# Weight-sum transfers in a one-core decoder trunk: plain copies on SyncE's queue, adds on GpSimd's, both held until 1/rms of their half

## The chip, the cores and the metric

The kernel runs on one core of one Trainium2 chip. The metric is the device time of one execution in microseconds (us), the median of the runs shown; lower is better.

## What is computed

One layer on x of shape (1, 2048, 1024), all in float32 (cut from the reference):

```python
h = rms_norm(x, norm1_g)
z = einsum('bsd,de->bse', h, w_in)            # 1024 -> 3584
lru_x, lru_gate, sc_b, sc_c, sc_x = split(z)
y_lru = rg_lru(causal_dwconv(lru_x, lru_conv_w) + lru_conv_b, ...) * gelu(lru_gate)
y_sc = sc_b * causal_dwconv(sc_c * sc_x, sc_conv_w)
x = x + einsum('bse,ed->bsd', concatenate([y_lru, y_sc]), w_out)
h = rms_norm(x, norm2_g)
gate, up = split(causal_dwconv(einsum('bsd,df->bsf', h, w_up), ffn_conv_w))
x = x + einsum('bsf,fd->bsd', gelu(gate) * up, w_down)
return rms_norm(x, final_g)
```

## The kernel before

Activations stand transposed, features on the 128 partitions and time along the free dimension. The 2048 positions are worked in two **halves** of 1024. Float32 products are made of three reduced-precision ones: `split` (L192 to L194) writes a high part with ScalarE and the rest with VectorE, and TensorE sums high x high, high x low and low x high.

The program goes through six stages in order: input phase of half 0 (`in_phase`, L403), output product of half 0 (`sweeps` named "o"), input phase of half 1, output product of half 1, then up product and down product of half 0, and up and down product of half 1. The order on TensorE (PE), SyncE (SP) and GpSimd (POOL) is that of the code; VectorE (DVE) and ScalarE (ACT) are ordered by a scheduler with priorities, so that an instruction more elsewhere can move theirs.

**Input phase.** It makes 28 input products a half, each of 48 matmuls of 128x512. `load_weights` puts the transfer of a product's weights (512 KB, `wr_in`, L211) on SP's queue into one of two raw buffers; eight of the products bring gate weights in the same raw buffer (L216), which stays taken until these are split. The products are not divided by the norm first: 1/rms of the half (`inv_rms`, L257 to L271, tile `ss_a`) is computed after the first products and multiplied in when a product leaves PSUM (`evac`, L362). What follows is convolution (L290, L292), gates (`zr`, `zi`), scan (L344), and stores of the result blocks to HBM (`y_d`, L190). `with_halo` and `keep_halo` (L276 to L283) are small GpSimd instructions that carry the last columns of a tile from half to half.

**Output and down product.** `sweeps` (L674) uses a Strassen-like scheme with seven block products instead of eight. Each sweep loads a weight block (L701) and a feature block (L702, from `y_d` or `f_d`), splits both, and runs 24 matmuls for each pair. In the output product of half 0, x of half 1 is loaded and prepared beside it (`x1_beside`, L391 to L393, `sq`, L246, L247); in that of half 1 it is the input of the up product (`h_beside`, L507). Both read 4 MB for this. The output product has 7 x 3 x 24 = 504 matmuls.

**Weight sums.** Four of the seven weight operands are sums of blocks: S1 = W21 + W22, S3 = W21 + W11, S2 = S1 + W11, S4 = S2 + W12. They are made by transfers from HBM to HBM of 512 KB each, without an engine: a plain copy into the sum's place (`so_d` for the output weights, `sd_d` for the down weights), then a transfer that adds the second operand there. There are 3 blocks a sum for `so_d` and 6 for `sd_d`, so 12 copies and 12 adds in half 0, and 24 and 24 in half 1. All are issued on GpSimd's queue in `in_product`, after each input product, one at a time in half 0 and two in half 1:

```python
for _ in range(min(half + 1 if o != 1 or half else 0, len(pieces))):   # L354
    dst, src, op = pieces.pop(0)
    nc.gpsimd.dma_start(dst, src, accum_op=op, max_dma_last_dim=2 * T)  # L356
```

`sums` (L662) makes the list `pieces`; that of the down weights is made right before the output product of half 0, so that its transfers belong to the input phase of half 1. GpSimd runs ahead of TensorE where nothing holds it.

Of the kernel before, what the change touches and what calls it, by code (L numbers as in the profile page):

```python
# [10 lines left out]
ALU = mybir.AluOpType  # L11
# [5 lines left out]
T = 1024  # L17
# [14 lines left out]
W_OPS = ["W21", "W11", "W22", "W12"]  # L32
# [19 lines left out]
]  # L52
PLACE = {"11": (0, 0), "12": (0, 1), "21": (1, 0), "22": (1, 1)}

SUMS = [("S1", "W21", "W22"), ("S3", "W21", "W11"), ("S2", "S1", "W11"), ("S4", "S2", "W12")]

O_G1, O_G2, O_GF = 0, 8, 16
O_LCW = 24
# [10 lines left out]
def block_kernel(  # L69
# [11 lines left out]
    nc = tc.nc  # L81
# [9 lines left out]
    ones = cp.tile([P, P], F32, name="ones")  # L91
# [22 lines left out]
    def col(o):  # L114
        return prm[:, o : o + 1]
# [4 lines left out]
    def act(name):  # L120
        return page(name, "act", 28)
# [4 lines left out]
    def tmp(name):  # L126
        return page(name, "tmp", 7)
# [7 lines left out]
    def pst(name):  # L135
        return pp.tile([P, NB], F32, name=name, tag="ps")
# [4 lines left out]
    def flat(t):  # L141
        return t.rearrange("p a b -> p (a b)")

    def r32(ap):
        return ap.bitcast(F32R)

    def blk(b):
        return slice(b * NB, (b + 1) * NB)
# [28 lines left out]

    waiting = []
    pieces = []

    def defer(n, dst, src):
        waiting.append([n, dst, src])
# [66 lines left out]
    def mean_split(acc, name):  # L249
        n = acc.shape[-1]  # L250
        hi = flat(tmp(f"rh_{name}"))[:, :n]
        lo = flat(tmp(f"rl_{name}"))[:, :n]
        with tc.high_priority(offset=HP):
            split(hi, lo, acc)
        return hi, lo

    def inv_rms(acc, name, parts=None):  # L257
        n = acc.shape[-1]
        terms = parts or mean_split(acc, name)
        pss = [pst(f"ms_{name}_{t}") for t in range(0, n, NB)]  # L260
        for i, x in enumerate(terms):
            for b, p in enumerate(pss):
                nc.tensor.matmul(p, ones_r, r32(x[:, blk(b)]), start=i == 0, stop=i == len(terms) - 1)
        with tc.high_priority(offset=HP):
            y = flat(tmp(f"ry_{name}"))[:, :n]
            for b, p in enumerate(pss):
                nc.scalar.activation(y[:, blk(b)], p, AF.Abs_reciprocal_sqrt, bias=eps)
                nc.vector.scalar_tensor_tensor(acc[:, blk(b)], p, EPS, y[:, blk(b)], ALU.add, ALU.mult)  # L268
            nc.vector.scalar_tensor_tensor(acc, acc, -0.5, y, ALU.mult, ALU.mult)
            nc.vector.scalar_tensor_tensor(acc, acc, 1.5, y, ALU.add, ALU.mult)  # L270
        return acc  # L271

    def with_halo(name, n, half, store, side):
        t = big(name, side)
        if half == 0:
            nc.gpsimd.memset(t[:, 0:n], 0.0)  # L276
        else:
            nc.gpsimd.tensor_copy(t[:, 0:n], store)
        return t

    def keep_halo(t, n, half, store):
        if half < NH - 1:
            nc.gpsimd.tensor_copy(store, t[:, T : T + n])  # L283
# [12 lines left out]
    def lru_conv(c, half, ps, rs):  # L296
        xl = with_halo(f"xl{half}_{c}", 3, half, xl_halo[:, c, :], c % 2)
        evac(xl[:, 3 : 3 + T], ps, rs)
        keep_halo(xl, 3, half, xl_halo[:, c, :])
        cv = flat(act(f"cv{half}_{c}"))  # L300
        conv(cv, xl, 4, O_LCW + 4 * c, bias=col(O_LCB + c))
        xc = (flat(act(f"xch{half}_{c}")), flat(act(f"xcl{half}_{c}")))
        split(xc[0], xc[1], cv)
        return xc, cv
# [22 lines left out]
    def lru_scan(c, half, cv, g, ps_r, ps_i):  # L327
# [20 lines left out]
        nc.vector.tensor_tensor(h, g, h, ALU.mult)  # L348
        return h

    def in_product(o, half, acts):
        ps = pst2(f"zin{half}_{o}")
        product(ps, load_weights(w_in[o], f"in{half}_{o}", o - NLRU if NLRU <= o < 2 * NLRU else None), acts)
        for _ in range(min(half + 1 if o != 1 or half else 0, len(pieces))):  # L354
            dst, src, op = pieces.pop(0)
            nc.gpsimd.dma_start(dst, src, accum_op=op, max_dma_last_dim=2 * T)  # L356
        return ps

    def evac(dst, ps, rs):
        with tc.high_priority(offset=HP):  # L360
            for b, p in enumerate(ps):
                nc.vector.tensor_tensor(dst[:, blk(b)], p, rs[:, blk(b)], ALU.mult)  # L362
# [40 lines left out]
    def in_phase(half, acts, acc, between):  # L403
# [19 lines left out]
        gw = gate_weights(0, half)  # L423
        ps_2 = in_product(1, half, acts) if half == 0 else None
        rs = inv_rms(acc, f"a{half}", parts)
        xc, cv = lru_conv(0, half, pss[0], rs)
        if half == 0:
            decay_rates()
# [231 lines left out]
            between(j)  # L660

    def sums(src, dst, n):  # L662
        for k in range(2 * len(SUMS)):
            o, a, b = SUMS[k // 2]
            for i2 in range(n // 2):
                t = flat(dst[o][i2])
                if k % 2 == 1:
                    pieces.append((t, src[W_OPS.index(b), i2], ALU.add))
                elif a in W_OPS:
                    pieces.append((t, src[W_OPS.index(a), i2], ALU.bypass))  # L670
                else:
                    pieces.append((t, flat(dst[a][i2]), ALU.bypass))

    def sweeps(half, wsrc, fsrc, ni, name, residual, done, beside, tail=0):  # L674
        keep = None
# [69 lines left out]
    ss1[0] = acc_tile("a0")  # L745
    sums(w_out, so_d, NO)
    in_phase(0, None, ss1[0], nothing)
    assert not pieces
    sums(w_down, sd_d, NI)

    x1 = []
# [240 lines left out]
```

## Time and profile before

| | |
|---|---|
| median of 3 runs (lowest to highest) | 2332.79 us (2329.52 to 2335.15) |
| the profiled execution | 2334.91 us, of which the span from first to last instruction 2333.1 us |
| TensorE busy, mean granted clock | 98% of the span, 0.989 |
| VectorE, ScalarE, GpSimd busy | 74%, 49%, 7% |
| transfers | 378.28 MB; SP's queue 41.8% and GpSimd's 7.5% of 16 engines' span |

Busy shares are of the whole span; a stage in which TensorE waits shows in the slices of the span and in tables by stretch. Queue q1 (hardware) is SP's, q0 (software) GpSimd's. A matmul's mean duration overlaps the next one's; the distance of two starts is what it costs.

### The profile page before, as it was taken

How to read it: one execution, taken by the hardware profiler on the slowest of the kernel's cores; microseconds unless marked ns; L12 is line 12 of the kernel's file. 1: busy time of each engine (PE TensorE's matmuls, PEld its weight loads, DVE VectorE, ACT ScalarE, POOL GpSimd, SP SyncE). 2: the span in 40 equal slices, each digit the busy share in tenths (PEclk: the TensorE clock that was granted, in tenths of full speed). 3: DMA queues.
4: the chain of work that ended last, by engine and by line, in shares of the span. 5: the costliest groups of instructions: out<-in, count | busy, mean ns of one | idle time of the engine just before them, and what ended most of it. 6: DMA issues, size and time to landing. Idle time of an engine off the chain costs nothing.

```text
span 2333.1 us, 26007 instructions
## 1 busy us (share of the span) xinstructions
PE 2283.3 (98%) x9984; PEld 1880.7 (81%) x9984; DVE 1724.3 (74%) x1910; ACT 1136.7 (49%) x1242; POOL 167.0 (7%) x266
## 2 busy tenths in 40 slices
PE   8999997999999999999999999999999999999997
PEld 7888885778888878888888888888888888887885
DVE  7656566757666699898887877677888887876656
ACT  5553464536525645554444454445454444443343
POOL 0001110101110000020111100000010001100000
PEclk9999998999999999999999999999999999999999
DMA  4344448966763288232323247576223232348754
GB/s 160 98 126 124 127 115 312 286 213 151 183 166 91 96 291 294 98 113 91 114 91 123 94 149 283 189 247 240 101 91 113 91 113 91 113 163 314 258 193 180
DMA packets 149629, 378.28 MB, mean 162 GB/s; under 512 B 13824, under 2 KB 17024, under 8 KB 149504
## 3 DMA queue, kind: packets, MB, share of 16 engines
q1 hardware_dynamic: 134528, 338.87, 41.8%
q0 software_dynamic: 14976, 37.75, 7.5%
q8 instruction: 78, 1.28, 0.2%
q14 instruction: 47, 0.39, 0.1%
HBM read 289.53 MB, written 124.78 MB: 178 GB/s over the span
## 4 chain that ended last, share of the span: by engine, by line
PE 74%; DMA 6%; DVE 6%; ACT 2%; issue 1%; SPq 0%; POOL 0%; DVEq 0%; ACTq 0%; POOLq 0%
PE zx L569 22%; PE zin_b L232 13%; PE zc L569 11%; PE dx L690 11%; PE dy L690 8%; PE za L569 6%; PE ox L690 1%; DMA wr_in<-in_w_in 1%; DMA x<-in_xT 1%; DVE fl_o L194 1%; DMA wr_o<-in_w_out 1%; DMA wr_o<-y_d_B 1%; DVE xr L727 1%; PE oy L690 1%; DMA wr_d<-sd_d_S 1%
## 5 line engine op out<-in xcount | busy, mean ns | idle before, releaser
L232 PE MATMUL zin_b<-xh,wh_in 128*128 128x512 f32 x896 | 277.5, 391 | 5.2 <-DVE ss_a L268 2.6
L232 PE MATMUL zin_b<-xl,wh_in 128*128 128x512 f32 x896 | 277.3, 391 | 0.5 <-DVE xl L393 0.5
L232 PE MATMUL zin_b<-xh,wl_in 128*128 128x512 f32 x896 | 277.1, 391 | 0.0
L232 PEld LDWEIGHTS zin_b<-xh,wh_in 128*128 128x128 f32 x896 | 169.1, 189 | 41.5 <-DVE ss_a L268 3.5
L232 PEld LDWEIGHTS zin_b<-xl,wh_in 128*128 128x128 f32 x896 | 168.5, 188 | 36.8 <-DVE xl L393 2.2
L232 PEld LDWEIGHTS zin_b<-xh,wl_in 128*128 128x128 f32 x896 | 168.9, 189 | 35.2
L193 ACT ACTIVATE fh_d<-wr_d 128x1024 fp32r<-128x1024 f32 x84 | 89.1, 1060 | 162.7 <-PE dx L690 80.4
L194 DVE TENSOR_TENSOR fl_d<-wr_d,fh_d 128x1024 fp32r<-128x1024 f32 x84 | 102.8, 1223 | 88.3 <-ACT fh_d L193 85.8
L194 DVE TENSOR_TENSOR wl_in<-wr_in,wh_in 128x1024 fp32r<-128x1024 f32 (+1 forms) x62 | 69.2, 1119 | 131.8 <-ACT wh_in L193 131.8
L193 ACT ACTIVATE wh_in<-wr_in 128x1024 fp32r<-128x1024 f32 (+1 forms) x62 | 60.2, 974 | 212.9 <-DMA wr_in<-in_w_in 212.7
L194 DVE TENSOR_TENSOR wla_up<-wr_up,wha_up 128x1024 fp32r<-128x1024 f32 x48 | 58.8, 1226 | 139.0 <-ACT wha_up L193 139.0
L690 PE MATMUL dx<-fl_d,wh_d 128*128 128x512 f32 x384 | 149.6, 390 | 0.8 <-DVE fl_d L194 0.8
L690 PE MATMUL dx<-fh_d,wh_d 128*128 128x512 f32 x384 | 149.4, 389 | 0.0
L690 PE MATMUL dx<-fh_d,wl_d 128*128 128x512 f32 x384 | 149.4, 389 | 0.0
L545 DVE TENSOR_TENSOR wr_up<-wr_up 128x512 f32<-128x512 f32 x192 | 130.0, 686 | 12.7 <-DMA wr_up<-in_w_up 11.5
L194 DVE TENSOR_TENSOR wl_d<-wr_d,wh_d 128x1024 fp32r<-128x1024 f32 x84 | 102.6, 1221 | 44.3 <-ACT wh_d L193 41.9
L569 PE MATMUL zc<-hhB,whd_up 128*128 128x512 f32 x384 | 126.0, 389 | 0.0
L292 DVE SCALAR_TENSOR_TENSOR cu<-un,prm,cu 128x1024 f32<-128x1024 f32 x96 | 122.7, 1278 | 4.3 <-ACT cu L288 4.3
L193 ACT ACTIVATE wh_d<-wr_d 128x1024 fp32r<-128x1024 f32 x84 | 88.5, 1053 | 74.4 <-DMA wr_d<-sd_d_S 43.5
L292 DVE SCALAR_TENSOR_TENSOR cg<-ug,prm,cg 128x1024 f32<-128x1024 f32 x96 | 122.8, 1279 | 0.4
L569 PE MATMUL zx<-ht,whc_up 128*128 128x512 f32 x384 | 118.2, 389 | 0.0
L580 ACT ACTIVATE ug<-zx 128x512 f32<-128x512 f32 x96 | 57.5, 599 | 120.0 <-PE zx L569 119.7
(256 smaller groups left out, 5631.2 us busy)
## 6 DMA issues: line engine op xcount, KB each, us to landing
wr_up<-in_w_up SPq DMA_DIRECT2D x96, 512.0 KB, 4.9
wr_in<-in_w_in SPq DMA_DIRECT2D x54, 512.0 KB, 4.1
wr_d<-sd_d_S SPq DMA_DIRECT2D x48, 512.0 KB, 3.9
wr_d<-f_d_T SPq DMA_DIRECT2D x48, 512.0 KB, 5.1
sd_d_S<-in_w_down POOLq DMA_DIRECT2D x36, 512.0 KB, 7.0
f_d_B<-cu SPq DMA_DIRECT2D x72, 256.0 KB, 2.4
wr_d<-in_w_down SPq DMA_DIRECT2D x36, 512.0 KB, 3.7
wr_d<-f_d_B SPq DMA_DIRECT2D x36, 512.0 KB, 4.7
```

The costliest lines, as they stand in the source:

```text
L193: nc.scalar.activation(r32(hi), src, AF.Copy)
L194: nc.vector.tensor_tensor(r32(lo), src, hi, ALU.subtract)
L232: nc.tensor.matmul(ps[t], r32(a), r32(b[:, blk(t)]), start=(first and i == 0), stop=(last and i == 2))
L292: nc.vector.scalar_tensor_tensor(dst, src[:, k : k + T], col(o_w + k), dst, ALU.mult, ALU.add)
L545: nc.vector.tensor_tensor(raw[:, o, :], raw[:, a, :], raw[:, b, :], ALU.add)
L569: nc.tensor.matmul(ps, r32(p[:, s]), r32(self.hs[k][x][o]), start=f and i == 0, stop=l and i == 2, skip_group_check=True,)
L580: nc.scalar.activation(dst, self.x, AF.Copy)
L690: nc.tensor.matmul(ps[m], r32(p), r32(x[:, k, :]), start=first and i == 0 and n == 0, stop=(last or not on_x) and i == ni - 1 and n == 2, ...
L727: nc.vector.tensor_tensor(r, r, ps[m], ALU.add if sign > 0 else ALU.subtract)
```

## The change

`sum_step` issues, after an input product, one plain copy on SP's queue and, two products later, its add on GpSimd's. It is called only once 1/rms of the half has been given out in the program (`ready`), and a one-column GpSimd copy that reads `rs` makes GpSimd's queue itself wait for that 1/rms. The operands of S2 and S4 change places, so that the plain copy comes from the weights and the add from the earlier sum. The numbers of copies and adds, and their bytes, stay.

```diff
--- before.py
+++ after.py
@@ -52,7 +52,7 @@
 ]
 PLACE = {"11": (0, 0), "12": (0, 1), "21": (1, 0), "22": (1, 1)}
 
-SUMS = [("S1", "W21", "W22"), ("S3", "W21", "W11"), ("S2", "S1", "W11"), ("S4", "S2", "W12")]
+SUMS = [("S1", "W21", "W22"), ("S3", "W21", "W11"), ("S2", "W11", "S1"), ("S4", "W12", "S2")]
 
 O_G1, O_G2, O_GF = 0, 8, 16
 O_LCW = 24
@@ -177,6 +177,8 @@
 
     waiting = []
     pieces = []
+    adds = []
+    ready = []
 
     def defer(n, dst, src):
         waiting.append([n, dst, src])
@@ -348,12 +350,19 @@
         nc.vector.tensor_tensor(h, g, h, ALU.mult)
         return h
 
+    def sum_step():
+        if pieces:
+            dst, src, add = pieces.pop(0)
+            nc.sync.dma_start(dst, src)
+            adds.append((dst, add))
+        if len(adds) > 2 or adds and not pieces:
+            nc.gpsimd.dma_start(*adds.pop(0), accum_op=ALU.add, max_dma_last_dim=2 * T)
+
     def in_product(o, half, acts):
         ps = pst2(f"zin{half}_{o}")
         product(ps, load_weights(w_in[o], f"in{half}_{o}", o - NLRU if NLRU <= o < 2 * NLRU else None), acts)
-        for _ in range(min(half + 1 if o != 1 or half else 0, len(pieces))):
-            dst, src, op = pieces.pop(0)
-            nc.gpsimd.dma_start(dst, src, accum_op=op, max_dma_last_dim=2 * T)
+        if len(ready) > half:
+            sum_step()
         return ps
 
     def evac(dst, ps, rs):
@@ -423,6 +432,8 @@
         gw = gate_weights(0, half)
         ps_2 = in_product(1, half, acts) if half == 0 else None
         rs = inv_rms(acc, f"a{half}", parts)
+        nc.gpsimd.tensor_copy(ones[:, 0:1], rs[:, 0:1])
+        ready.append(True)
         xc, cv = lru_conv(0, half, pss[0], rs)
         if half == 0:
             decay_rates()
@@ -660,16 +671,11 @@
             between(j)
 
     def sums(src, dst, n):
-        for k in range(2 * len(SUMS)):
-            o, a, b = SUMS[k // 2]
+        for o, a, b in SUMS:
             for i2 in range(n // 2):
                 t = flat(dst[o][i2])
-                if k % 2 == 1:
-                    pieces.append((t, src[W_OPS.index(b), i2], ALU.add))
-                elif a in W_OPS:
-                    pieces.append((t, src[W_OPS.index(a), i2], ALU.bypass))
-                else:
-                    pieces.append((t, flat(dst[a][i2]), ALU.bypass))
+                add = src[W_OPS.index(b), i2] if b in W_OPS else flat(dst[b][i2])
+                pieces.append((t, src[W_OPS.index(a), i2], add))
 
     def sweeps(half, wsrc, fsrc, ni, name, residual, done, beside, tail=0):
         keep = None
@@ -745,7 +751,6 @@
     ss1[0] = acc_tile("a0")
     sums(w_out, so_d, NO)
     in_phase(0, None, ss1[0], nothing)
-    assert not pieces
     sums(w_down, sd_d, NI)
 
     x1 = []
```

**GpSimd, between the last unit of half 0 and the first products of half 1.** `h_last`, `p_halo` and `xl_halo` are halo copies; `sd_d` are the sums of the down weights. Before:

```order
L346 COPY h_last<-r_7_2423 128x1
L356 DMA so_d_S_2_222<-in_w_out 256x512
L276 MEMSET pr_3_2502 128x2
L283 COPY p_halo<-pr_3_2502 128x2
L356 DMA sd_d_S_0_223<-in_w_down 256x512
L356 DMA sd_d_S_1_224<-in_w_down 256x512
L356 DMA sd_d_S_2_225<-in_w_down 256x512
L356 DMA sd_d_S_3_226<-in_w_down 256x512
L278 COPY xl_0_3637<-xl_halo 128x3
L356 DMA sd_d_S_4_227<-in_w_down 256x512
L356 DMA sd_d_S_5_228<-in_w_down 256x512
```

After the change:

```order
L348 COPY h_last<-r_7_2425 128x1
L278 MEMSET pr_3_2503 128x2
L285 COPY p_halo<-pr_3_2503 128x2
L435 COPY ones<-ss_a_2579 128x1
L280 COPY xl_0_3635<-xl_halo 128x3
L280 COPY xl_1_3782<-xl_halo 128x3
L359 DMA sd_d_S_0_223<-in_w_down 256x512
L359 DMA sd_d_S_1_224<-in_w_down 256x512
L280 COPY pr_0_3980<-p_halo 128x2
```

The last add of `so_d` has moved up by half a phase, and the copy that reads `ss_a` (1/rms of half 1) now stands ahead of every transfer of `sd_d`.

**SP, the first products of half 1** (`wr_in` are weight loads). Before:

```order
L211 DMA wr_in_1_3655<-in_w_in 128x1024
L211 DMA wr_in_9_3713<-in_w_in 128x1024
L216 DMA wr_in_9_3713<-in_w_gate 128x256
L211 DMA wr_in_20_3821<-in_w_in 128x1024
L211 DMA wr_in_24_3928<-in_w_in 128x1024
```

After:

```order
L213 DMA wr_in_1_3653<-in_w_in 128x1024
L356 DMA sd_d_S_0_223<-in_w_down 16x8192
L213 DMA wr_in_9_3710<-in_w_in 128x1024
L218 DMA wr_in_9_3710<-in_w_gate 128x256
L356 DMA sd_d_S_1_224<-in_w_down 16x8192
L213 DMA wr_in_20_3817<-in_w_in 128x1024
```

One copy, of 16 rows of 32 KB, stands between two weight loads; on GpSimd a transfer was cut into 256 rows of 2 KB.

**VectorE, 1/rms of half 0 and the first convolution** (`wl_in` are low parts of weights, `xl_0` to `xcl_0` the first unit). Before:

```order
L194 TENSOR_TENSOR wl_in_24_818<-wr_in_24_816,wh_in_24_817 128x1024
L268 SCALAR_TENSOR_TENSOR ss_a_271<-ms_a_0_539,ry_a_545 128x512
L269 SCALAR_TENSOR_TENSOR ss_a_271<-ss_a_271,ry_a_545 128x1024
L270 SCALAR_TENSOR_TENSOR ss_a_271<-ss_a_271,ry_a_545 128x1024
L194 TENSOR_TENSOR wl_in_16_881<-wr_in_16_879,wh_in_16_880 128x1024
L362 TENSOR_TENSOR xl_0_552<-zin_0_b_272,ss_a_271 128x512
L292 SCALAR_TENSOR_TENSOR cv_0_557<-xl_0_552,prm,cv_0_557 128x1024 x2
L194 TENSOR_TENSOR wl_in_2_946<-wr_in_2_944,wh_in_2_945 128x1024
L292 SCALAR_TENSOR_TENSOR cv_0_557<-xl_0_552,prm,cv_0_557 128x1024
L194 TENSOR_TENSOR xcl_0_563<-cv_0_557,xch_0_562 128x1024
```

After:

```order
L270 SCALAR_TENSOR_TENSOR ss_a_271<-ms_a_0_539,ry_a_545 128x512
L271 SCALAR_TENSOR_TENSOR ss_a_271<-ss_a_271,ry_a_545 128x1024
L196 TENSOR_TENSOR wl_in_24_819<-wr_in_24_817,wh_in_24_818 128x1024
L272 SCALAR_TENSOR_TENSOR ss_a_271<-ss_a_271,ry_a_545 128x1024
L371 TENSOR_TENSOR xl_0_553<-zin_0_b_272,ss_a_271 128x512
L294 SCALAR_TENSOR_TENSOR cv_0_558<-xl_0_553,prm,cv_0_558 128x1024
L196 TENSOR_TENSOR wl_in_16_883<-wr_in_16_881,wh_in_16_882 128x1024
L294 SCALAR_TENSOR_TENSOR cv_0_558<-xl_0_553,prm,cv_0_558 128x1024 x2
L196 TENSOR_TENSOR xcl_0_564<-cv_0_558,xch_0_563 128x1024
```

The low parts of products 24 and 16 now stand later, among 1/rms and the convolution, and that of product 2 behind `xcl_0`. TensorE's own order is the same in both kernels.

## Rows read from the trace of the kernel before

**Rows 1.** The page's busy time of TensorE and its granted clock in 40 slices.

```profile
PE 2283.3 (98%) x9984; PEld 1880.7 (81%) x9984; DVE 1724.3 (74%) x1910; ACT 1136.7 (49%) x1242; POOL 167.0 (7%) x266
...
PEclk9999998999999999999999999999999999999999
```

**Rows 2.** Stretches of both output products: length, busy us of each engine, PEclk, DMA share, GB/s.

```profile
344.85:490.99 146.14, 124.88 (x506) 99.46 (x505) 100.51 (x106) 65.16 (x64) 16.28 (x23) 0.91 0.91 298
819.20:940.41 121.21, 116.76 (x505) 95.61 (x504) 115.06 (x131) 60.93 (x63) 0.33 (x4) 0.99 0.80 288
```

**Rows 3.** Waits of TensorE, output product of half 0: total us, times, longest.

```profile
PE ox L690 <- ACT fh_o L193: 8.4, 1, 8.4
PE oy L690 <- ACT fh_o L193: 6.9, 2, 4.3
```

**Rows 4.** Queues in the output product, first two half 0, last half 1.

```profile
q1 hardware_dynamic: 11813, 34.51, 65.9%
q0 software_dynamic: 3394, 8.93, 24.9%
...
q1 hardware_dynamic: 12220, 34.80, 79.2%
```

**Rows 5.** GpSimd's transfers by time in the output product of half 0.

```profile
348.98 0.59 POOL L356 DMA_DIRECT2D sd_d_S<-in_w_down  x1
355.09 1.13 POOL L356 DMA_DIRECT2D sd_d_S<-in_w_down  x2 [5.52 <-issue]
356.90 0.56 POOL L356 DMA_DIRECT2D sd_d_S<-in_w_down  x1 [0.68 <-issue]
...
483.88 0.56 POOL L356 DMA_DIRECT2D sd_d_S<-in_w_down  x1 [0.62 <-issue]
```

**Rows 6.** TensorE by time: start, us; three without a wait, three after one.

```profile
344.85 0.39 PE L690 MATMUL ox<-fh_o,wh_o 128*128 128x512 f32 x1
...
350.29 0.39 PE L690 MATMUL ox<-fh_o,wh_o 128*128 128x512 f32 x1
...
365.21 0.80 PE L690 MATMUL ox<-fh_o,wh_o 128*128 128x512 f32 x1 [8.39 <-ACT fh_o L193]
...
388.43 0.79 PE L690 MATMUL oy<-fh_o,wh_o 128*128 128x512 f32 x1 [4.30 <-ACT fh_o L193]
...
398.56 0.39 PE L690 MATMUL ox<-fh_o,wh_o 128*128 128x512 f32 x1
...
478.76 0.79 PE L690 MATMUL ox<-fl_o,wh_o 128*128 128x512 f32 x1 [2.63 <-DVE fl_o L194]
```

**Rows 7.** Store of the last scan, median us to landing: half 0, then half 1.

```profile
y_d_B<-r SPq DMA_DIRECT2D x1, 256.0 KB, 7.2
...
y_d_B<-r SPq DMA_DIRECT2D x1, 256.0 KB, 2.3
```

**Rows 8.** GpSimd's queue in 538 to 572 us (six adds), then 572.4 to 597 (copies).

```profile
q0 software_dynamic: 1480, 3.05, 55.3%
...
q0 software_dynamic: 1136, 3.67, 50.5%
```

**Rows 9.** Input phase of half 1: the stretch; adds of 538 to 572 us, us to landing.

```profile
490.00:820.00 330.00, 330.00 (x1458) 273.25 (x1457) 213.90 (x219) 169.12 (x173) 30.09 (x41) 1.00 0.51 137
...
sd_d_S<-in_w_down POOLq DMA_DIRECT2D x6, 512.0 KB, 6.2
```

**Rows 10.** Start of half 0 by time: weight loads on SP, VectorE, TensorE.

```profile
37.61 0.33 SPq L211 DMA_DIRECT2D wr_in<-in_w_in  x1
...
43.53 0.33 SPq L211 DMA_DIRECT2D wr_in<-in_w_in  x1
...
47.62 1.23 DVE L269 SCALAR_TENSOR_TENSOR ss_a<-ss_a,ry_a 128x1024 f32<-128x1024 f32 x1
...
53.83 2.60 DVE L292 SCALAR_TENSOR_TENSOR cv<-xl,prm,cv 128x1024 f32<-128x1024 f32 x2 [0.20 <-ACT cv L290]
...
61.18 0.73 PE L232 MATMUL zr_b<-xcl,gw 128*128 128x512 f32 x2 [0.52 <-DVE xcl L194]
```

## Prediction

> **What bounds the kernel now.** I read the page's shares first: TensorE is busy for 2283.3 of 2333.1 us, so all its idle time is 49.8 us, and the one slice with a lower granted clock than the others is the seventh, 350 to 408 us [rows 1]. That points to one place, the output product of half 0. The table by stretch sets it beside its twin in half 1 [rows 2]. The reader should see that both have the same 504 matmuls, that one takes 146.14 us and the other 121.21, and that GpSimd is busy in the first alone. Matmuls that wait for nothing start 24 in 350.29 - 344.85 = 5.44 us, 0.2267 each [rows 6], so the work is 504 x 0.2267 = 114.3 us. The first sweep set loses 31.9 us (21.3 idle, 146.14 - 124.88, and 10.6 at a lower clock or while it comes back); the second loses 6.9.
>
> What TensorE waits for there is the high part of a feature block, once 8.4 us and twice more for 6.9 us together [rows 3]. Behind such a split stands a load, and the queues tell why it is late: SP's queue takes 65.9% of 146.14 = 96.3 us of all 16 engines in half 0, and 79.2% of 121.21 = 96.0 in half 1 [rows 4]. The kernel's own loads and stores are the same work. What half 0 has besides is GpSimd's queue, 24.9% = 36.4 us. Together that is 133 us of transfers under 114 us of matmuls; in half 1 it is 96 under 114. These transfers are sums of the **down** weights, 16 of them between 348.98 and 483.88 us [rows 5], whose readers come hundreds of us later. Nothing asks for them then; GpSimd merely had nothing ahead of them that waits.
>
> Elsewhere TensorE does not wait for transfers: in the stretch of half 1's input phase it is busy 330.00 of 330 us [rows 9].
>
> **The change part by part.** *The sums leave the output product of half 0.* In the order of GpSimd the copy that reads 1/rms of half 1 stands ahead of the first `sd_d` transfer, and TensorE makes the sums of squares for that 1/rms only after two products of half 1. So no add can start before the sweeps end; the copies on SP stand behind the third weight load of half 1, so they can't either. The `so_d` adds end in the middle of half 0's phase instead of at its end. All of GpSimd's 36.4 us leave the stretch, and its load becomes that of the twin.
>
> Taken from the twin alone, the gain is 146.14 - 121.21 = 24.9 us. I take less, since one cause of waiting is the half's own: the last scan's result is stored and read back at once. That store took 7.2 us to land in half 0, 2.3 in half 1 [rows 7]. With the twin's 2.3 the wait of 8.39 us at 365.21 [rows 6] shrinks by 4.9 to 3.5, but half 1 has none there. So the stretch comes to 121.2 + 3.5 = 124.7 us, **a gain of 21.4**. On one side VectorE has less to do beside these sweeps than beside the twin's (100.51 against 115.06 us of busy time [rows 2]), so the loss could fall to some 4 us: a gain of 28. On the other side the first waits could stay (second rival).
>
> *The copies on SP's queue.* There are 36, 12 in half 0 and 24 in half 1, one between two weight loads. A copy takes of the queue: 50.5% of 24.6 us for 3.67 MB, seven transfers, so 1.77 us each; an add 55.3% of 34 us for six, 3.1 us each [rows 8]. In half 1 the sums thus ask for 24 x (1.77 + 3.1) = 117 us of a phase of about 330. The busiest case for a load is where gate weights hold one of the two raw buffers and each load waits for the split before it: then loads follow each other in 43.53 - 37.61 = 5.92 us [rows 10], while TensorE uses one per 48 x 0.2267 = 10.88. The cover is 4.96 us a product. A copy of 1.77 fits, and it runs mostly while the load ahead of it is split: **cost 0**. The row that I price by is that of the same copies on the other queue; in 16 rows of 32 KB no row of before shows one. Bounds: below, nothing (a gain is excluded where TensorE never waits); above, 6.2 us, as long as an add takes to land [rows 9], which is the slower rival.
>
> The Trainium skill speaks against this move (DMA: Bandwidth & Descriptors, section on queues, rings and completion order): an engine takes turns between the rows of different queues packet by packet, but works off one queue's ring in its order, so a load on SP's queue waits for all of a copy ahead of it, where GpSimd's copy would only have interleaved. By the row a copy delays the load by at most 1.77 us and the sum keeps its 0; by the rule the delay is the whole copy, however long it is, which raises the chance of the slower rival and changes the sum only past 4.96 us. The trace of before has no copy from HBM to HBM on SP's queue, so it can't decide this.
>
> *GpSimd's wait.* Behind the copy that waits for 1/rms are the halo instructions of the first unit. In half 0 the first convolution's VectorE taps start at 53.83 us, while 1/rms is complete about 51 us (L269 ends at 48.85, and L270 and one low part of 1.23 us follow [rows 10]); a one-column copy and a memset fit into the 2.5 us between. In half 1 two products (21.8 us) lie between 1/rms and the first gates. Cost 0; without that cover, some 1 us. GpSimd has 36 transfers fewer to issue, which nobody waits for.
>
> *VectorE's new order at the start.* The low part of product 24 moves behind L269, from before 43.53 (when the load of product 16 that reused its buffer was issued) to about 50.0 us. The load of 16 follows at 50.1, 6.6 later, and its low part now stands between the taps of the first convolution, where product 2's stood. The copy ahead can add 1.77. The gates wait for that chain already, 0.52 us at 61.18 [rows 10]. Carried through (the load as long as before or 1.77 longer, its two splits, two taps, one split), it ends 0 to 1.5 us later than before: **cost 0.8**. Other splits move inside the input phases too; there TensorE waited for none [rows 9], and weights are split ahead of their product.
>
> *Sum:* -21.4 + 0.8 = -20.6 us. The profiled execution took 2334.91 (span 2333.1), 2.1 above the median 2332.79; the cut goes alike from all. 2332.8 - 20.6 = **2312 us**.
>
> **The rivals.**
>
> *Half of it.* The first two sweeps read blocks that were stored just before, and load the residuals beside; if their waits come from that alone, they stay. They last from 344.85 to 398.56, 53.7 us for 144 matmuls worth 32.6 [rows 6], a loss of 21.1. Only the remaining 31.9 - 21.1 = 10.8 us, less some 2 that the twin loses late too, would go: 2332.8 - 9 + 0.8 = 2325 us. For it: the wait at 388.43 comes when the four early sums should have landed. Against it: the twin has the same stores and residuals there, and loses 6.9 in all.
>
> *No change (2330 us, 0 to 4.7 under).* The loads of the sweep fill the engines anyway, and preparing x on ScalarE holds the splits back; or the sums, pushed out, come back at another place, such as the second output product. Against it: equal 96 us on SP's queue in both, and in the changed order the last `sd_d` copy stands on SP's queue ahead of the phase's last two weight loads, its add right behind the last halo copy of the phase.
>
> *Slower.* The copies starve the weight loads. Place: both input phases; mechanism: SP's queue serves a copy of 16 long rows before the next load, and loads in the single-buffered stretches can't be sent ahead. Price: (copy - 4.96) x 36. It cancels the gain from 4.96 + 20.6 / 36 = 5.5 us a copy. With 6.2 us it is 45 us: 2332.8 - 20.6 + 44.6 = 2357 us. For it: nothing measured the 32 KB rows. Against it: the same bytes took 1.77 us of the engines in rows of 2 KB. The rule of the skill named above is this rival's rule.
>
> **How the numbers follow.** Forecast 0.74, half 0.13, no change 0.07, slower 0.06. Differences within 0.2%, 4.7 us, a measurement of this kernel can't tell from none (its three runs spread by 0.24%). Faster by over 0.2%: 0.74 + 0.13 = 0.87; within: 0.07; slower: 0.06. The forecast's own range is a gain of 28 to 14 us (3.5 us for the first wait doubled, 1.5 us at the start and 2 for added splits off), 2305 to 2319. To leave out no more than 2 in 10 it reaches to the half: 2305 to 2326.
>
> **What would show it right or wrong.** Right: GpSimd's queue moves nothing between the last product of half 0 and the first of half 1; the output product of half 0 takes 118 to 128 us with SP's queue still at 96 us of it; the store of the last scan lands in 2 to 4 us; TensorE's granted clock in that stretch is 0.97 or more; the input phases keep TensorE without waits after their start, with the first gates up to 1.5 us later. Wrong: waits of input products for weight splits (slower rival), a wait of 4 us or more for a feature block before 400 us (half), or adds of `sd_d` under the second output product.

## The result and the profile after

The changed kernel takes **2314.59 us** (median of 4 runs, 2311.53 to 2315.52), the kernel before in the same job 2333.97 (2329.52 to 2339.1). The ratio is 0.9914, with a 95% interval of 0.9891 to 0.9937: faster by some 19 to 20 us. The profiled execution took 2314.18 us, with a span of 2312.4.

First the page's busy time and granted clock; they answer to [rows 1].

```profile
PE 2278.3 (99%) x9984; PEld 1879.7 (81%) x9984; DVE 1724.5 (75%) x1910; ACT 1135.9 (49%) x1242; POOL 143.7 (6%) x232
...
PEclk9999999999999999999999999999999999999998
```

The low slice at 350 to 408 us is gone. The table by stretch has the output product of half 0, the input phase of half 1 and the output product of half 1 (columns as in [rows 2]).

```profile
345.36:468.79 123.43, 117.42 (x505) 96.43 (x504) 93.96 (x101) 63.18 (x63) 0.00 (x0) 0.97 0.78 276
468.79:797.01 328.22, 328.22 (x1450) 271.79 (x1448) 213.03 (x217) 168.10 (x172) 27.84 (x37) 1.00 0.60 161
797.01:920.60 123.59, 118.57 (x505) 96.68 (x504) 115.86 (x132) 61.40 (x63) 0.33 (x4) 0.97 0.79 284
```

The first output product lost 146.14 - 123.43 = 22.7 us and is now like its twin. GpSimd does nothing in it. The input phase of half 1 takes 328.22 us, as it did before (490.99 to 819.20, 328.21 us), with TensorE never idle. The second output product is 2.4 us longer than in [rows 2]; over the kernels below that put no more transfers on a queue, it takes 121.6 (half 1 as before) to 124.7 us, so this can't be told from scatter. The start of the first output product, 345.36 against 344.85, can't either: over the kernels below that make half 0's sums in either of these two ways it begins anywhere from 344.4 to 347.5 us.

The queues in the output product of half 0, then in the input phase of half 1, with median landing times:

```profile
q1 hardware_dynamic: 11634, 34.02, 78.2%
...
q1 hardware_dynamic: 11913, 39.90, 35.6%
q0 software_dynamic: 6528, 12.58, 24.0%
...
wr_in<-in_w_in SPq DMA_DIRECT2D x26, 512.0 KB, 4.3
sd_d_S<-in_w_down SPq DMA_DIRECT2D x24, 512.0 KB, 5.4
```

SP's queue has 78.2% of 123.43 = 96.5 us in the first stretch, as in [rows 4]; GpSimd's queue has no line there. TensorE's waits of over half a microsecond that are left in that stretch, by time:

```profile
377.34 0.49 PE L696 MATMUL oy<-fh_o,wh_o 128*128 128x512 f32 x1 [4.62 <-ACT fh_o L195]
...
379.23 0.80 PE L696 MATMUL oy<-fl_o,wh_o 128*128 128x512 f32 x1 [1.39 <-DVE fl_o L196]
```

The wait of 8.39 us at 365 of [rows 6] is gone altogether; the one at 388 is still there, as 4.62 us at 377. The chain of work shows why the first went: the last scan is stored 6.5 us earlier (342.52 against 349.05), and its store lands in 2.52 us where it took 7.23. First two rows before the change, then two after it:

```profile
349.05 7.23 DMA y_d_B<-r
...
356.30 7.72 DMA wr_o<-y_d_B
...
342.52 2.52 DMA y_d_B<-r
...
345.11 8.63 DMA wr_o<-y_d_B
```

The load behind the store thus lands 10.3 us sooner (353.74 against 364.02): 6.5 from the earlier store, 4.7 from its landing, less 0.9 by which the load itself is longer.

### The profile page after: what moved, and what is told of

Read it like the earlier page. It is cut to its first block, busy times and chain, and to the rows that moved or that the text cites. A ratio compares the mean times of both kernels' runs of the same rounds, so it can differ in the third digit from the quotient of the medians.

```text
span 2312.4 us, 26025 instructions
## 1 busy us (share of the span) xinstructions
PE 2278.3 (99%) x9984; PEld 1879.7 (81%) x9984; DVE 1724.5 (75%) x1910; ACT 1135.9 (49%) x1242; POOL 143.7 (6%) x232
## 4 chain that ended last, share of the span: by engine, by line
PE 86%; DVE 5%; DMA 5%; ACT 3%; issue 1%; SPq 0%; POOL 0%; DVEq 0%; ACTq 0%; POOLq 0%
PE zx L580 23%; PE zin_b L234 20%; PE zc L580 11%; PE dx L696 11%; PE dy L696 8%; PE za L580 6%; PE ox L696 3%; PE oy L696 3%; DMA wr_in<-in_w_in 1%; DMA wr_o<-y_d_B 1%; PE zr_b L234 1%; PE zi_b L234 1%; DMA x<-in_xT 1%; DMA wr_d<-sd_d_S 0%; DVE fl_o L196 0%
```

## The experiments

Twelve kernels were run. All diffs are against the changed kernel.

**The two halves of the change apart.** Each of two kernels makes the change in one half and keeps the old list of pieces (`pieces_old`), one or two transfers a product on GpSimd's queue, in the other, where the one-column copy is left out too. The diffs show only where the transfers are issued.

```diff
 e1_so_early, in in_product:
-        if len(ready) > half:
+        if half == 1:
+            for _ in range(min(2, len(pieces_old))):
+                dst, src, op = pieces_old.pop(0)
+                nc.gpsimd.dma_start(dst, src, accum_op=op, max_dma_last_dim=2 * T)
+        elif ready:
             sum_step()
 e2_sd_held, in in_product:
-        if len(ready) > half:
+        if half == 0:
+            for _ in range(min(0 if o == 1 else 1, len(pieces_old))):
+                dst, src, op = pieces_old.pop(0)
+                nc.gpsimd.dma_start(dst, src, accum_op=op, max_dma_last_dim=2 * T)
+        elif len(ready) > 1:
             sum_step()
```

> Half 0 as in the changed kernel (sums of the output weights ready by its middle, copies on SP's queue); half 1 as before: two transfers a product on GpSimd's queue, nothing held. Theory A (the gain is the transfers of the down sums leaving the output product of half 0): they are in it again, 16 of them and some 36 us of the engines' time, so that stretch loses most of what it gained; only the early last scan is kept, which by the wait of 8.39 us at 365 is at most some 8 us of it. Output product of half 0 at 135 to 146 us, total 2325 to 2335 us. Rival B (the gain is that the last scan of half 0 ends 6.5 us earlier, because the sums of the output weights are ready long before): the stretch stays at 123 to 127 us, total 2313 to 2318 us, although the same 16 transfers run under it.

> Half 0 as before (one transfer a product on GpSimd's queue, to the end of the phase); half 1 as in the changed kernel (held until 1/rms of half 1, copies on SP's queue). Theory A: the transfers of the down sums are gone from the output product of half 0, so most of the gain is there; the last scan ends late again (its store issued near 349 us), so the first wait for a feature block near 365 us is back with 3 to 8 us. Output product of half 0 at 125 to 131 us, total 2315 to 2322 us. Rival B: without the early scan the gain is gone, 140 us or more and 2328 us or more. With the run that does only the other half the two parts should add up to the whole, some 20 us.

Measured: 2329.47 us (0.9975, 0.9964 to 0.9987) with half 0 alone changed, 2319.57 us (0.9928, 0.9912 to 0.9945) with half 1 alone, the kernel before at 2335.30: gains of 5.8 and 15.7, together 21.5, about the whole. (The profile of the first fell on a run of 2324.65, 4.8 under its median.) The stretch of the first, with GpSimd's queue in it and the landing of the last scan's store; then that of the second, with that store and the wait for its block:

```profile
345.42:480.93 135.51, 122.41 (x506) 98.14 (x504) 93.58 (x100) 62.39 (x61) 12.57 (x16) 0.95 0.92 307
...
q0 software_dynamic: 2751, 7.21, 21.6%
...
y_d_B<-r SPq DMA_DIRECT2D x1, 256.0 KB, 6.9
```

```profile
344.42:474.86 130.44, 120.53 (x505) 97.72 (x504) 101.39 (x108) 66.00 (x66) 2.34 (x4) 0.95 0.78 271
...
348.21 5.79 DMA y_d_B<-r
...
360.63 0.80 PE L715 MATMUL ox<-fh_o,wh_o 128*128 128x512 f32 x1 [4.64 <-ACT fh_o L196]
```

Theory A holds for the larger part: with the down sums in it the stretch takes 135.51 us, without them 130.44 or 123.43. But the other half is a gain of its own. Where the sums of the output weights run to the end of half 0, the last scan is stored at 348.21, its store takes 5.79 us to land, and 4.64 us of waiting follow even with the down sums gone. Where they are over by the middle, the store starts at 341.31 and 342.52, and no wait at the head of the stretch is over 0.8, although with the down sums in the stretch the store takes 6.9 us. So it is the earlier scan, more than the shorter landing, that ends the first wait.

Why the scan is earlier, the waits of ScalarE for weight loads late in half 0 show, first before the change, then after it:

```profile
256.11 1.06 ACT L193 ACTIVATE wh_in<-wr_in 128x1024 fp32r<-128x1024 f32 x1 [8.85 <-DMA wr_in<-in_w_in]
...
281.30 1.06 ACT L193 ACTIVATE wh_in<-wr_in 128x1024 fp32r<-128x1024 f32 x1 [16.10 <-DMA wr_in<-in_w_in]
...
253.21 1.06 ACT L195 ACTIVATE wh_in<-wr_in 128x1024 fp32r<-128x1024 f32 x1 [4.17 <-DMA wr_in<-in_w_in]
...
274.58 1.06 ACT L195 ACTIVATE wh_in<-wr_in 128x1024 fp32r<-128x1024 f32 x1 [12.27 <-PE zin_b L234]
```

Before the change seven transfers of `so_d` start between 245 and 287 us, after it none. The split that is 6.7 us later (281.30 against 274.58) holds up ScalarE's work behind it, and the last scan is 6.6 us later (344.29 against 337.74). TensorE waits for none of this inside the phase.

**Extra transfers under the twin.**

```diff
+                n = {0: 4, 2: 12}.get(at.index(s), 0) if half == 0 else 0
+                if n:
+                    nc.gpsimd.tensor_copy(ones[:, 0:1], hs[half][-1]["T4"][0][:, 0:1])
+                for i in range(n):
+                    k = len(spares)
+                    spares.append(dr.tile([P, 2, NB], F32, name=f"spare{k}"))
+                    nc.gpsimd.dma_start(flat(spares[-1]), w_down[k % 4, k // 4], accum_op=ALU.bypass, max_dma_last_dim=2 * T)
```

> The changed kernel, with 16 more plain copies of down weights of 512 KB on GpSimd's queue under the output product of half 1 (into spare memory that nothing reads), released by work of that stretch in a group of 4 and a group of 12. Theory A (an output product whose own transfers take some 96 us of its 114 us of matmuls has no room for more): it loses what the other output product gained. By the price of 1.77 us a copy that the trace of before shows they ask for 28 us, 10 more than there is room for; they stand in two bursts, so that stretch grows from 123.6 by 8 to 25 us, total 2322 to 2340 us. Rival (the first output product was slow for reasons of its own, the stored blocks and the late scan): the second grows by less than 4 us.

```profile
796.23:934.01 137.78, 123.56 (x506) 99.23 (x505) 115.53 (x131) 61.80 (x63) 12.63 (x22) 0.93 0.86 314
...
q0 software_dynamic: 2304, 8.39, 16.9%
```

2328.12 us (0.9971, 0.9958 to 0.9984), 13.5 over the changed kernel, and the stretch is 14.2 longer than 123.59; the longest new wait is 7.62 us for a feature block at 899.50, inside the burst of twelve. So the other output product had no room for such transfers either: 16.9% of 137.78 = 23.3 us of them cost 14.2.

**The hold and the queue.** The change holds GpSimd with a copy that reads 1/rms, and moves the plain copies to SP's queue. Which of them matters? One kernel lacks the first, three lack the second.

```diff
 e4_no_hold_copy:
-        nc.gpsimd.tensor_copy(ones[:, 0:1], rs[:, 0:1])
 e3_held_gpsimd (half 0 as before), in in_product:
+        elif len(ready) > 1:
+            for _ in range(min(2, len(pieces_old))):
+                dst, src, op = pieces_old.pop(0)
+                nc.gpsimd.dma_start(dst, src, accum_op=op, max_dma_last_dim=2 * T)
 e10_held_long_rows, e3 with:
+                if op == ALU.bypass:
+                    nc.gpsimd.dma_start(dst, src)
 e12_only_queue, in sum_step:
-            nc.sync.dma_start(dst, src)
+            nc.gpsimd.dma_start(dst, src, accum_op=ALU.bypass, max_dma_last_dim=2 * T)
```

> The changed kernel without the one-column copy on GpSimd that waits for 1/rms; everything else as changed. The adds then are held only by the copies on SP's queue that they add to, and these stand behind weight loads that can't be issued before the sweeps of half 0 end. If it is this order that keeps the sums out of the output product, nothing changes: 2311 to 2317 us, no transfer of a down sum between 345 and 468 us. If the wait for 1/rms is what holds them, they are back in the stretch and the time is 2322 us or more.

> As the run with the down sums alone held, but with their plain copies left on GpSimd's queue, two transfers a product: the wait without the second queue. Copies of half 1 then cost 1.77 us each of the engines' time as before the change, not the 1.41 that SP's queue showed; both fit beside the matmuls. Theory C (the other queue matters little for the time, the wait makes the gain): the same as that run within 4 us, 2315 to 2324 us. Theory D (one queue can't finish 48 transfers between 1/rms of half 1, about 500 us, and the end of the phase at 797 us, since they land one behind another in some 6 us each, 288 us): the last of them run into the output product of half 1 and it grows beyond 123.6 us by up to 10 us.

> The run with all 48 down sums held and left on GpSimd's queue, with their plain copies in rows of 32 KB. That run lost 11 us in the input phase of half 1, where gate weights were split late in two units (5.61 us of waiting at 707 us). Theory E (what cost there is that the transfers run back to back on one queue beside the weight loads, whatever their rows): the phase stays at 335 us or more, total 2328 to 2335 us. Theory F (the short rows of the copies take the engines' time, 0.36 us each more): with long rows the phase comes back to 328 to 330 us, total 2319 to 2323 us, as with the copies on SP's queue.

> The changed kernel with one thing put back: the plain copies go on GpSimd's queue (2 KB rows as before the change), each at the same product and two pieces ahead of its add as now. Theory G (the copies on SP's queue stand between two weight loads and are paced by them, and each add waits for its copy; on GpSimd's queue all 48 run back to back beside the loads): the phase of half 1 grows by 8 to 18 us, with gate weights split late, as in the two runs with everything held on GpSimd's queue; total 2322 to 2333 us. Theory C (the queue of the copies doesn't matter, and those two runs were slow by their order of transfers, the add right behind its own copy): the phase stays at 328.2 us, total 2312 to 2317 us.

Without the hold: 2314.06 us (0.9907, 0.9892 to 0.9922), the same as with it. GpSimd's first add of a down sum then starts here, in the input phase and 20.6 us before its 500.80 in the changed kernel, after a wait for its own copy:

```profile
480.24 0.89 POOL L359 DMA_DIRECT2D sd_d_S<-in_w_down  x1 [53.94 <-DMA sd_d_S<-in_w_down]
```

So the wait for 1/rms does nothing for the time as long as the copies stand on SP's queue.

With the copies on GpSimd's queue the gain is lost: 2331.68 us with that one line put back (0.999, 0.9972 to 1.0008; its ten runs lie between 2321.49 and 2339.85, and its profile is of one of 2327.30), 2333.12 with half 1 alone held (0.9986, 0.9975 to 0.9997), and 2339.91 with long rows (1.0016, 1.0005 to 1.0027). Theories C and F fall; that the last sums would spill into the next stage (theory D) falls too, since every transfer starts before it. What E and G expected of the place holds: in all three, the output product of half 0 stays short (124.07 us in the kernel with one line put back, 130.96 and 131.49 in the two whose half 0 is as before, near the 130.44 above), and the input phase of half 1 grows: 333.62, 339.22 and 346.47 us against 328.22. Their sizes missed: G had the phase 8 to 18 us longer and it is 5.4; E had 2328 to 2335 us in all. In the first of these three half 0's phase is also 6 us longer. The wait is for gate weights that are split late; the first stretch and the wait are those of the kernel with one line put back, then come the stretches of the other two:

```profile
475.51:809.13 333.62, 330.05 (x1450) 272.73 (x1448) 210.01 (x214) 167.62 (x171) 41.67 (x61) 0.99 0.59 157
...
701.49 0.79 PE L234 MATMUL zr_b<-xch,gw 128*128 128x512 f32 x1 [3.57 <-ACT gw L195]
...
477.40:816.62 339.22, 332.04 (x1449) 273.48 (x1448) 211.84 (x217) 167.48 (x171) 41.20 (x61) 0.99 0.60 155
...
476.95:823.42 346.47, 333.46 (x1449) 274.99 (x1448) 211.56 (x217) 167.45 (x171) 41.70 (x61) 0.98 0.57 152
```

The amount over the phase doesn't tell them apart. Over the phase both queues together take 24.0% + 35.6% of 328.22 = 195.6 us in the changed kernel and 34.1% + 24.8% of 333.62 = 196.5 with the line put back. What differs first is when they run. The queues in the first 165 us of the phase, for the kernel before, the changed one and the one with the line put back:

```profile
q0 software_dynamic: 5043, 12.74, 36.1%
q1 hardware_dynamic: 5412, 13.24, 23.7%
...
wr_in<-in_w_in SPq DMA_DIRECT2D x15, 512.0 KB, 4.3
```

```profile
q1 hardware_dynamic: 5904, 21.24, 37.2%
q0 software_dynamic: 3575, 6.90, 26.6%
...
wr_in<-in_w_in SPq DMA_DIRECT2D x16, 512.0 KB, 4.2
```

```profile
q0 software_dynamic: 6944, 17.83, 47.9%
q1 hardware_dynamic: 5296, 13.11, 24.1%
...
wr_in<-in_w_in SPq DMA_DIRECT2D x15, 512.0 KB, 5.1
```

Counted from the rows by time, the transfers of down sums started in the first 145 us of the phase are 24 before (16 more had run under the output product), 24 in the changed kernel, and 34, 30 and 32 in the three. By 165 us they are 24, 30, and 34, 33 and 35, so that the distance is largest in between. With the line put back a load then lands in 5.1 us instead of 4.2, and the splits behind it fall back. In us from the start of the phase, from ScalarE's rows by time, the start of some weight splits (the first counted is the one some 7 us before the phase), and of the split of the gate weights that the wait above is for. Where TensorE doesn't wait, it comes to these gates at 222.1. The last column is a kernel of the next group, with each copy on SP's queue issued twice:

| split | before | changed | line put back | half 1 alone held | copies twice |
|---|---|---|---|---|---|
| 11th | 94.8 | 90.9 | 98.1 | 99.2 | 94.2 |
| 14th | 126.7 | 123.4 | 130.9 | 130.6 | 128.3 |
| 18th | 172.8 | 169.7 | 175.8 | 183.6 | 176.8 |
| 19th | 193.6 | 191.9 | 198.1 | 204.5 | 196.5 |
| 20th | 200.4 | 198.4 | 206.1 | 212.4 | 204.8 |
| gate weights | 218.0 | 212.9 | 225.5 | 229.9 | 219.3 |

Where three loads follow each other, each waiting for the split before it, they take this long with the line put back, from the chain of work; behind them the changed kernel's ScalarE by time, whose first two loads, of 657.19 and 663.04 us, are there after 3.50 and 4.15 us:

```profile
668.53 5.05 DMA wr_in<-in_w_in
...
676.00 5.53 DMA wr_in<-in_w_in
...
683.96 7.84 DMA wr_in<-in_w_in
```

```profile
660.69 1.06 ACT L195 ACTIVATE wh_in<-wr_in 128x1024 fp32r<-128x1024 f32 x1 [2.77 <-DMA wr_in<-in_w_in]
667.19 1.06 ACT L195 ACTIVATE wh_in<-wr_in 128x1024 fp32r<-128x1024 f32 x1 [5.44 <-DMA wr_in<-in_w_in]
```

The third load is no faster in the changed kernel: issued at 669.54 us, it lands after 8.69. But nothing stands behind it there. Moving the copies has changed ScalarE's order as well, which the scheduler makes. In the kernel before, and in every kernel here without copies on SP's queue in half 1, the split of this load comes ahead of the gates (L335 to L339) and of the split of their weights; with copies on SP's queue it comes behind them. First two rows with the line put back, where the gates wait 8.07 us with it, then two of the changed kernel:

```profile
691.89 1.06 ACT L195 ACTIVATE wh_in<-wr_in 128x1024 fp32r<-128x1024 f32 x1 [8.07 <-DMA wr_in<-in_w_in]
...
701.04 0.40 ACT L195 ACTIVATE gw<-wr_in 128x256 fp32r<-128x256 f32 x1
...
681.65 0.40 ACT L195 ACTIVATE gw<-wr_in 128x256 fp32r<-128x256 f32 x1
...
682.91 1.04 ACT L195 ACTIVATE wh_in<-wr_in 128x1024 fp32r<-128x1024 f32 x1
```

Late splits alone don't make the wait either, as the table shows. With each copy issued twice the 20th split is 1.3 us ahead of the one with the line put back, but the order is the changed kernel's, the gate weights are split at 219.3 us, and no matmul of the phase waits. The old order alone costs nothing either: the kernel before, with fewer transfers by then, split them at 218.0. So this wait came of both, splits that fell back and one of them ahead of the gates. No run changes one of the two and leaves the other, with the same 48 transfers.

What the SP queue gives is thus a pace, and an order that came with it. There a copy stands between two loads, and comes no earlier than the load before it may be issued; an add waits for its copy, up to 25 us:

```profile
623.27 0.89 POOL L359 DMA_DIRECT2D sd_d_S<-sd_d_S  x1 [25.16 <-DMA sd_d_S<-in_w_down]
```

On its own queue GpSimd issues as fast as transfers land: with the line put back, between 512 and 595 us, nearly every one starts some 0.3 us after another has landed, with two under way. The queue by itself does no harm: the kernel before ran 24 in 145 us on GpSimd's queue alone, in the old order, and lost nothing. GpSimd's queue held to that pace after the sweeps was not tried, and why long rows made it 6.8 us worse than short ones stays open.

**More copies on SP's queue, and their rows.**

```diff
 e7_copies_x2, e8_copies_x4 (n = 1, 3):
+            for _ in range(n):
+                spare = dr.tile([P, 2, NB], F32, name=f"spare{len(spares)}")
+                spares.append(spare)
+                nc.sync.dma_start(flat(spare), src)
 e9_sp_short_rows:
-            nc.sync.dma_start(dst, src)
+            nc.sync.dma_start(dst, src, max_dma_last_dim=2 * T)
```

> The changed kernel with each plain copy on SP's queue issued twice (the second into spare memory): 36 more of them, 1.41 us of the engines each by the trace of the changed kernel, so 2.8 us a product where the prediction's cover is 4.96 us. By that cover no change: 2312 to 2318 us, no wait of an input product for a split. If a copy ahead of a load delays it by its whole landing time of 5.4 us and two by 10.8, loads fall behind in the single-buffered stretches and it costs up to (10.8 - 5.4) x 36 = 194 us.

> The changed kernel with each plain copy on SP's queue issued four times: 5.6 us a product by 1.41 us each, over the cover of 4.96 us. By the cover a loss of (5.64 - 4.96) x 36 = 24 us, and the engines' time in the input phase of half 1 comes to 116.8 + 78.8 + 72 x 1.41 = 297 of 328 us, near full, so loads also land later: 2330 to 2380 us, with input products waiting for weight splits. If it costs nothing, the cover is larger than the prediction's.

> The changed kernel with the plain copies on SP's queue in rows of 2 KB, as GpSimd's queue had them before, in place of 32 KB. It separates the rows from the queue. If the length of the rows makes the copy cheaper (1.41 us of the engines on SP's queue against 1.77 on GpSimd's), the price goes back to some 1.8 us a copy, the time stays within 3 us of the changed kernel (under the cover of 4.96 us). If it is the queue, the price stays at 1.4 us.

Measured: 2321.85 us with two copies (0.9953, 0.9935 to 0.9971), 2356.36 with four (1.0096, 1.0067 to 1.0125), 2313.11 with short rows (0.9915, 0.9889 to 0.9942). SP's queue and the weight loads in the input phase of half 1, with two and with four, then SP's queue with short rows:

```profile
q1 hardware_dynamic: 12448, 52.04, 44.9%
...
wr_in<-in_w_in SPq DMA_DIRECT2D x26, 512.0 KB, 5.8
```

```profile
q1 hardware_dynamic: 13984, 77.21, 61.1%
...
wr_in<-in_w_in SPq DMA_DIRECT2D x26, 512.0 KB, 7.9
```

```profile
q1 hardware_dynamic: 17785, 40.13, 37.0%
```

Against 35.6% of 328.22 that makes (147.4 - 116.8) / 24 = 1.27 us a copy for the second, (214.5 - 116.8) / 72 = 1.36 for the next three, and (121.4 - 116.8) / 24 = 0.19 more for short rows. So the short rows cost about half of the difference to 1.77, and nothing in time. Twice the copies cost half 1's phase nothing (328.21 us), but the first output product starts 3.6 us later, and both output products are longer by 2.6 and 5.9 us; I had expected no change, and 7.3 us came (the profile fell on the slowest of its runs, 2326.14). Why the output products grew was not followed up. Four copies cost 14.8 us in half 0's phase and 22.8 in half 1's, 37.6 where the cover of 4.96 us a product gave 24. The cover was taken from one pair of loads at the start of half 0; for all 36 it was too large, by (37.6 - 24) / 36 = 0.4 us a product. The slower rival's mechanism is real, at a price that this change doesn't reach.

A load on SP's queue lands in 4.3, 5.8 and 7.9 us with one, two and four copies between loads, 1.5 and then 1.05 us more for each further copy, near a copy's own 1.3. The Trainium skill (DMA: Bandwidth & Descriptors, section on queues, rings and completion order) has an engine work off a queue's ring in order, and take turns between queues. These numbers agree with the first; on the turns they say nothing, since loads and copies are on one queue.

**What waits at 377 us.** The split of x on ScalarE stands ahead of the split that ends the last two waits, and its load takes 8.89 us from 364.39. Two kernels load x later.

```diff
 e6_x_later:
-        if s % 2 == 0 and 2 <= s <= 2 * KC:
+        if s % 2 == 0 and 4 <= s <= 2 * KC + 2:
 e11_x_skip:
+        if s == 2 or s % 2 == 0 and 6 <= s <= 2 * KC + 2:
```

> The changed kernel with the loads of the residual x beside the output sweeps two steps later, so that they don't stand between the store of the last block and the loads of features that read it. What is left of waiting in the output product of half 0 is 4.62 and 1.39 us, at 377 and 379 us. If those two come from a load of x that lands late in 8.9 us, ahead of the split of the feature block on ScalarE, they go: output product 117 to 120 us, and 2308 to 2312 us in all. If they come from the store that lands late, nothing changes, 2314 us. If x itself then comes late for the sums that use it, a new wait of some us appears.

> The changed kernel with the second and later loads of the residual x beside the sweeps two steps later; the first stays where it is. In the run with all of them later a load of x was still issued at 364 us, when the store that frees its buffer had landed, and the split of x stood ahead of the weight split on ScalarE until 373 us. Here no split of x stands there, so if that order on ScalarE makes the remaining wait of 4 to 6 us at 377 us, it goes: output product of half 0 at 117 to 120 us, total 2308 to 2312 us. If another load lands late there too, it stays at 2314 us.

2316.73 us (0.9925, 0.9908 to 0.9942) and 2312.58 us (0.9906, 0.9892 to 0.9921): neither is a gain that can be told from the changed kernel. In the first, a load of x was still issued at 363.83 and landed 9.07 us later. In the second, with none there, the chain goes through the feature block itself:

```profile
361.04 6.54 DMA y_d_T<-yd
...
367.60 8.90 DMA wr_o<-y_d_T
```

My cause was wrong: 3.04 and 0.76 us of waiting are left without it. In the changed kernel all that is loaded behind the burst of six block stores of 357 to 361 us, up to 370 us, takes 6.8 to 10.5 us, whatever it is. That this burst makes the wait is argued from these times; no run moves the stores.

## Why the prediction was right, and where it wasn't

- **The output product of half 0**: right in size, 22.7 us against the 21.4 forecast, with SP's queue still at 96.5 us. The cause is right for the larger part: with the down sums alone gone the whole gains 15.7 us. Held up from both sides, by the run that leaves the sums there and by the one that puts copies into the twin.
- **What stays of the first wait**: put at 3.5 us, by the shorter landing of the store. It went to nothing. With the down sums alone gone, 4.64 us stayed, and the store landed in 5.79 us and not in the twin's 2.3, so leaving the stretch didn't bring the step that I priced. What failed is that the `so_d` sums ending "in the middle of half 0's phase" was told and given no worth: without them beside the late weight loads of half 0 the last scan is stored 6.5 us earlier. That half of the change is worth 5.8 us by the run with half 0 alone changed.
- **The copies on SP's queue, cost 0**: right for the time. The price was 1.3 to 1.4 us, under the 1.77 that I took. The cover was some 14 us too generous in all with four copies, and with two, well under it, 7.3 us came where it gave none.
- **The sums in half 1, "117 us of a phase of about 330"**: the sum of engine time proved nothing. The same bytes, and 196 to 201 us on the queues, cost 5 to 18 us more where GpSimd issued them alone. I took the move to SP's queue for a risk only; it is what makes the postponed sums fit, by its pace and by ScalarE's new order. That order the prediction passed over with "other splits move inside the input phases too". Without the move there is no gain.
- **GpSimd's wait, cost 0**: right, and more: the wait is not needed at all.
- **The start, +0.8**: 0.5 measured, within scatter. The gates that were later are those of the second unit (75.95 us, a wait of 1.32 where 0.45 was), not the first, which still wait 0.53.
- **The rivals**: half of it asked for waits that stay at 388 us; one did (4.62 us at 377), which the prediction had listed as a sign against it (4 us or more before 400 us), but the rest went, and the stretch of 123.43 us decides for the forecast. No change is what the kernels with the copies on GpSimd's queue show, by another road than I gave: the sums came back as late gate weights in the input phase.

The sum was -20.6, the profiled executions differ by 2334.91 - 2314.18 = 20.7, the medians of the job by 19.4. So close a fit is luck: the first wait went by a part of the change that had no price, a wait of 4.62 us at 377 stayed that was not in the sum, and the second output product came out 2.4 us longer.

## What to carry to other kernels

When transfers are moved out of a full stage, look at the rate at which their new place will issue them, in its tightest stretch, and not at whether their sum fits the phase. Here GpSimd's queue, with nothing to wait for, issued as fast as transfers landed, and a copy between two loads on the loads' own queue came no faster than they did. Compare the order of the engines that a scheduler arranges, too: here a line that moves copies to another queue also moved weight splits on ScalarE, and a load of 8 us held up the gates in one order and nothing in the other. And ask of transfers that end earlier what ran slower beside them: here it was weight loads late in half 0, and by them the last scan.

## What was not expected of the hardware

A plain copy of 512 KB from HBM to HBM took 1.3 to 1.4 us of the engines in rows of 32 KB on SP's queue and 0.2 more in rows of 2 KB. An add of the same size on GpSimd's queue took 24.0% of 328.22 us / 24 = 3.28 us, more than twice that. Weight loads of the same size beside 72.0% of busy engines landed 0.9 us later than beside 63.8%, and TensorE waited in a phase that it had bounded. It didn't wait there with each copy issued twice, where loads landed in 5.8 us: the landing time alone doesn't tell.
